# Partial chunks of keys filled up with zeros to 128 rows in two attentions' weighted sums of values

## The chip, the cores and the metric

The kernel runs on one core of a Trainium2 chip. The metric is the device time of one launch in microseconds (us); lower is better. The core's engines are called as in the profile: PE (TensorE) multiplies, and PEld is its loading of weights, which can overlap the multiplying; DVE (VectorE), ACT (ScalarE) and POOL (GpSimd) work on tiles; SP starts most of the transfers. Each engine takes its own instructions in order and waits for the others by semaphores.

## The reference, cut to what matters

A first layer (a gated delta rule with convolutions and an MLP) is followed by two layers of attention with squared-ReLU MLPs, over 528 tokens (16 meta tokens and 512 others). Only the two attentions are touched. The first is sparse: each query keeps its 256 best keys by an index (here as a bias of -1e30 on the others).

```
s = jnp.einsum('qgrd,qkgd->qgrk', q_blk, k_sel) * scale
s = jnp.where(valid[:, None, None, :], s, -jnp.inf)
p = jax.nn.softmax(s, axis=-1)
return jnp.einsum('qgrk,qkgd->qgrd', p, v_sel)      # the weighted sum of values
```

The second is the forgetting attention: 16 heads, all earlier keys, with a running sum of log decays in the logits, and again a softmax and a weighted sum of the values. Everything is float32, to float32 accuracy.

## The kernel before

Matmuls take float32r operands, each matrix split into a high and a low part (wh and wl of weights, xh and xl of inputs), or plain float32, where one product is two records in the trace. A matmul's shape in the trace begins with the active rows of the array and its columns: `64*128` has 64 rows, which is the number of keys over which it sums.

**Sparse attention** (`Dsa.attend`). An item is a block b of 32 tokens times 4 heads (128 queries on the partitions) and a group g of keys' heads; there are 17 blocks and 4 groups, so 68 items. `probs` makes logits on PE (L1315, L1316), adds bias and finds minima on DVE (L1318), and takes exponentials on ACT (L1323) into the tile `pr` [128 queries, keys], of which there are three buffers. `values`, two items later, transposes `pr` by chunks of 128 keys on PE (L1339), copies the transposes out of PSUM on ACT into `pT` (full chunks by L1342, a partial chunk by L1344), and sums weights times values over the chunks on PE (L1349). Block b sees 32 (b + 1) keys, so its last chunk has 32, 64, 96 or 128 rows in turn; the last block has 528 keys and a last chunk of 16. Blocks 0 to 3 have one chunk, 4 to 7 two, and so on. Meanwhile DVE still finds the best keys of the last rows (`index`, L1279 and L1280), PE does the output products of the first tokens (`out`, L99) from item 40 on, and at item 38 `finish` transposes factors (L182), copies them (L1060, ACT) and multiplies the residual by them in eight instructions on POOL (L1072).

**Forgetting attention** (`Fox.attend`). An item is a pair of heads j, a pair of query tiles u, a head of the pair `par` and a tile r of 128 queries. Keys are cut so that chunk 0 is the 16 meta tokens and the other four are 128 each. `values(j, u, par)` runs 8 x 2 x 2 = 32 times: it transposes weights of 256 queries (L1653, always 128 columns, of which chunk 0 uses 16), splits them into the tiles pTh and pTl (L106 on ACT, L107 on DVE), and multiplies both with the values `V` (L1664). `prepare` makes `V` of the next pair of heads, in two buffers. PE does products of the next pair of heads (L99) in between.

The order of each engine's instructions is set by a scheduler in the building of the program, from the order in the code, priorities and a model of times; it can change wherever an instruction is added.

Of the kernel before, what the change touches and what calls it, by code (L numbers as in the profile page):

```python
# [28 lines left out]
# chunks of tokens: the partitions of a column, where each starts and how many of its tokens count  # L29
# [4 lines left out]
# columns of the packed per-partition parameters  # L34
# [12 lines left out]
class K:  # L47
    """The kernel's context: engines, pools and the pieces that recur."""

    def __init__(self, tc):  # L50
        self.tc = tc
        self.nc = tc.nc
        self.whole = False  # whether a bank takes all the tokens where it can
        self.low = None  # the engine of the weights' lower parts

    def psum(self, **banks):
        """A pool of PSUM banks, so many a tag, for a phase."""
        self.banks = banks
        assert sum(banks.values()) <= 8
        return self.tc.tile_pool(name="pm", bufs=1, space=PSUM)  # L60
# [4 lines left out]
    # ---------------------------------------------------------------- dense  # L65
    def load(self, wdram, kt=8, m=128):
        """Loads a block of kt tiles of weights for m outputs."""
# [5 lines left out]
    def weights(self, wdram, kt=8):  # L73
        """A block of kt tiles of weights, split into two float32r parts that sum to it exactly."""
        return self.weight_parts(self.load(wdram, kt), kt)
# [10 lines left out]
    def dense(self, wdram, xh, xl, evac, kt=8, lo=0, n=T):  # L86
        """One block of 128 outputs for n tokens, a bank of them at a time: evac(products, tokens) takes them over."""
# [14 lines left out]
    def split(self, hi, lo, src, w=None):  # L102
        """hi + lo = src (times w, a value per partition)."""
# [8 lines left out]
    def operand(self):  # L112
        """Two float32r tiles for the parts of a layer's input; the last ones' readers are done."""
        return [self.big.tile([128, KT, T], F32R, name=n, tag=n) for n in ("bigh", "bigl")]

    def operand2(self):
        """Another such pair."""
# [6 lines left out]
    # ---------------------------------------------------------------- 1 / sqrt  # L124
    def rsqrt(self, pool, out, ms, scale, eps, shape, tag, bufs=2):
        """out = (ms * scale + eps) ** -0.5 by an integer first guess and three Newton steps."""
# [21 lines left out]
    def squares(self, tiles, pool=None, lo=0, eng=None):  # L148
        """Sums over the tiles of their squares from token lo on, [128, tokens] with zeros around."""
# [15 lines left out]
    def sumsq(self, acc, chunks):  # L165
        """The sums over the partitions too, as columns of PSUM (a column a chunk of tokens)."""
# [7 lines left out]
    def rows(self, cols, chunks, take, tags=("pa", "pa")):  # L174
        """The transposes of cols(chunk) [tokens, 128], to take(values, tokens)."""
# [26 lines left out]
def delta_constants(k, pool):  # L202
    nc = k.nc
    # tri[d][j, i] = 1 where token j counts in the running sum of token i
# [15 lines left out]
# -------------------------------------------------------------------- first layer  # L220
# blocks of w_in: a head's q, k, v, then z, sc_b, sc_c, sc_x, gate_a, gate_b
# [9 lines left out]
class Layer1:  # L231
# [13 lines left out]
    def normed(self, out, lo=0):  # L245
        """Takes over the products of the tokens from lo on with their norm."""
# [4 lines left out]
    def start(self):  # L251
        """The input times the norm's weights, the tokens' factors of the norm, which follow the products, and the first blocks."""
        k, nc, s, io, xh, xl = self.k, self.nc, self.s, self.io, self.xh, self.xl
        # where the recurrence's tiles will be
# [39 lines left out]
    def gates(self):  # L294
        """Log decays, their running sums by chunks and betas."""
# [7 lines left out]
        with tc.tile_pool(name="l1g", bufs=1) as pg:  # L303
            G = self.G  # rows 0..15 beta, 32..47 decay; no decay where there is no token
# [99 lines left out]
    # ---- towards the merge  # L404
    def load_u(self):
        """The convolved branch in two parts, where the recurrence's tiles were."""
# [16 lines left out]
    def sc_out(self, j):  # L423
        """2 sigmoid(gate_b) y_b for 128 features, in place of the gate."""
# [7 lines left out]
    # ---- independent of the recurrence  # L432
# [7 lines left out]
    def conv_branch(self, j):  # L440
        """sc_b * conv(sc_c * sc_x) for 128 features, in three steps."""
# [27 lines left out]
    # ---- gated delta rule  # L469
    def setup(self):  # L470
        k, nc, tc, p = self.k, self.nc, self.tc, self.p
        # masks of the blocks that the first level of the inverse adds, for Q = (W N)^T: block b of Q's columns keeps the
        # rows of the sibling of that block
# [15 lines left out]
        # tokens from NM - 4 on, and one of none  # L489
# [7 lines left out]
    def stage_a(self, h):  # L497
        """Projections, convolutions and silu of one head: 2 silu of k and q by chunks, and of v."""
# [3 lines left out]
        for kind in "kqv":  # L502
            x = self.xp[self.xi % 3]
            self.xi += 1
            # queries count from token NM on (and float32r takes an even number of tokens)
# [30 lines left out]
    def stage_b(self, h, st):  # L536
        """Token-major k and -v, decays, the triangular systems and the inverses of their diagonal blocks."""
# [64 lines left out]
    def levels(self, h, st):  # L602
        """The inverses, block by block, doubled up to the chunk's size."""
# [17 lines left out]
        # blocks of 16: W += W N W between siblings, by way of Q = (W N)^T with a mask  # L621
# [21 lines left out]
        def turn(d, rows, cols):  # L643
            """A block of V as the transpose of W's."""
# [5 lines left out]
        # larger ones start at partitions that a product can take by itself  # L650
        for lv in LEVELS[1:]:
# [3 lines left out]
            def products(d, out, rows, cols, lhs, rhs, eng, pairs=None):  # L655
                """out[rows, cols] = lhs^T rhs for the pairs of blocks."""
# [24 lines left out]
    def stage_c(self, h, st):  # L681
        """The recurrences over the chunks in both directions, the norm and the gate of the output."""
# [54 lines left out]
        # with o = sum / sqrt(128) rq:  o rsqrt(mean(o^2) + eps)  # L737
# [27 lines left out]
def softplus(k, pool, y, A, n):  # L765
    """max(y, 0) + log1p(exp(-|y|)), the log by the series of 2 atanh(e / (2 + e))."""
# [1004 lines left out]
def fcol(v):  # L1771
    """[n * 128] -> [128, n]"""
    return np.asarray(v, np.float32).reshape(-1, 128).T
# [81 lines left out]
```

## Time and profile before

| what | value |
|---|---|
| times of three runs | 2604.51, 2614.54, 2614.96 us (median 2614.54) |
| span of the profiled execution | 2607.7 us |
| busy share of the span | PE 97%, PEld 89%, DVE 59%, ACT 41%, POOL 17% |
| sparse attention, `attend` | about 1365 to 1493 us of the span |
| forgetting attention, `attend` | about 1994 to 2224 us |

The profiled execution is one of its own; its time beside the span is not among the three, and the median stands 6.8 us above that span. Times in the trace count from the start of the span. A matmul's end is modelled, so the step from one start to the next tells more than its length. A granted clock of 1.00 is 2.4 GHz, 0.50 is 1.2 GHz.

### The profile page before, as it was taken

The page shows a single profiled execution, that of the slowest core. Times are in us where ns is not written, and L with a number is a line of the kernel's source. Part 1 is how long each engine was busy: PE and PEld are TensorE (multiplying, and loading weights), DVE is VectorE, ACT ScalarE, POOL GpSimd, SP SyncE. Part 2 cuts the span into 40 slices and gives each one's busy share as a digit, 9 for nine tenths or more (in the row PEclk, how much of TensorE's full clock was granted, in tenths as well). Part 3 has the DMA queues.
Part 4 walks back from the last instruction along what each step waited for, and adds up shares of the span by engine and source line. Part 5 has one row for each costly group of instructions (what it writes and reads, how often), then busy time and mean ns, then how long its engine had stood idle before and what let it go on. Part 6 is the DMA issues. An engine that isn't in the chain of part 4 may idle for free.

```text
span 2607.7 us, 45619 instructions
## 1 busy us (share of the span) xinstructions
PE 2523.1 (97%) x18012; PEld 2315.5 (89%) x18012; DVE 1535.0 (59%) x3288; ACT 1072.2 (41%) x2191; POOL 438.4 (17%) x599
## 2 busy tenths in 40 slices
PE   8899999999999999999879999999999999999999
PEld 8889999999899888888868999999999988788887
DVE  7878788766554444335998454244555767642432
ACT  5434445353423322333546543133334766431331
POOL 2322212100002111013641010000112444100000
PEclk9999999999999999999978999999999989999999
DMA  4334333524552332333321232223333222232332
GB/s 152 94 95 121 84 96 90 118 89 133 169 204 89 97 97 92 96 90 109 87 71 39 62 114 90 90 89 95 119 95 97 83 72 65 90 95 91 97 105 81
DMA packets 139206, 257.20 MB, mean 99 GB/s; under 512 B 65536, under 2 KB 69664, under 8 KB 138992
## 3 DMA queue, kind: packets, MB, share of 16 engines
q1 hardware_dynamic: 82176, 236.46, 29.2%
q10 hardware_dynamic: 56816, 17.82, 3.5%
q8 instruction: 142, 2.33, 0.4%
q14 instruction: 72, 0.59, 0.1%
HBM read 223.39 MB, written 22.34 MB: 94 GB/s over the span
## 4 chain that ended last, share of the span: by engine, by line
PE 79%; DVE 11%; DMA 3%; ACT 2%; issue 1%; POOL 0%; ACTq 0%; SPq 0%; DVEq 0%; POOLq 0%
PE ps_pd L99 46%; PE ps_pd L948 19%; PE ps_pa L1349 2%; PE ps_po L1664 2%; PE ps_pb L662 1%; DVE prod L839 1%; DVE wl L83 1%; PE ps_pt L1653 1%; PE ps_pt L1339 1%; DVE sc L1280 1%; DVE sc L1268 1%; DMA Dn<-gsc 1%; DVE m L1279 1%; DVE t L1086 1%; DMA blk<-nd 1%
## 5 line engine op out<-in xcount | busy, mean ns | idle before, releaser
L82 ACT ACTIVATE wh<-wr 128x1024 fp32r<-128x1024 f32 (+2 forms) x367 | 379.4, 1034 | 966.7 <-PE ps_pd L99 470.1
L99 PE MATMUL ps_pd<-bigh,wh 128*128 128x256 f32 (+5 forms) x2256 | 695.5, 310 | 17.7 <-ACT bigh L109 6.5
L99 PE MATMUL ps_pd<-bigh,wl 128*128 128x256 f32 (+5 forms) x2256 | 692.5, 308 | 5.4 <-DVE wl L83 5.4
L99 PE MATMUL ps_pd<-bigl,wh 128*128 128x256 f32 (+5 forms) x2256 | 692.5, 308 | 1.2 <-DVE bigl L110 1.0
L83 DVE TENSOR_TENSOR wl<-wr,wh 128x1024 fp32r<-128x1024 f32 (+2 forms) x355 | 429.1, 1209 | 314.9 <-ACT wh L82 308.8
L99 PEld LDWEIGHTS ps_pd<-bigh,wh 128*128 128x128 f32 (+1 forms) x2256 | 430.8, 191 | 39.5 <-ACT bigh L109 6.7
L99 PEld LDWEIGHTS ps_pd<-bigh,wl 128*128 128x128 f32 (+1 forms) x2256 | 430.9, 191 | 24.0 <-DVE wl L83 6.8
L99 PEld LDWEIGHTS ps_pd<-bigl,wh 128*128 128x128 f32 (+1 forms) x2256 | 431.0, 191 | 20.4 <-DVE bigl L110 3.0
L99 PE MATMUL ps_pd<-xh,wh 128*128 128x264 f32 (+1 forms) x1040 | 327.4, 315 | 1.2 <-ACT t L1544 1.2
L99 PE MATMUL ps_pd<-xh,wl 128*128 128x264 f32 (+1 forms) x1040 | 326.4, 314 | 0.8 <-DVE wl L83 0.8
L99 PE MATMUL ps_pd<-xl,wh 128*128 128x264 f32 (+1 forms) x1040 | 325.8, 314 | 0.0
L948 PE MATMUL ps_pd<-fh,wh 128*128 128x264 f32 (+1 forms) x944 | 315.6, 334 | 0.0
L948 PE MATMUL ps_pd<-fh,wl 128*128 128x264 f32 (+1 forms) x944 | 315.6, 334 | 0.0
L948 PE MATMUL ps_pd<-fl,wh 128*128 128x264 f32 (+1 forms) x944 | 315.4, 334 | 0.0
L99 PEld LDWEIGHTS ps_pd<-xh,wh 128*128 128x128 f32 x1040 | 196.7, 189 | 13.8 <-ACT t L1544 2.1
L99 PEld LDWEIGHTS ps_pd<-xh,wl 128*128 128x128 f32 x1040 | 196.8, 189 | 12.7 <-DVE wl L83 1.3
L99 PEld LDWEIGHTS ps_pd<-xl,wh 128*128 128x128 f32 x1040 | 196.9, 189 | 11.7
L948 PEld LDWEIGHTS ps_pd<-fh,wl 128*128 128x128 f32 x944 | 177.2, 188 | 19.5
L948 PEld LDWEIGHTS ps_pd<-fh,wh 128*128 128x128 f32 x944 | 177.2, 188 | 19.5
L948 PEld LDWEIGHTS ps_pd<-fl,wh 128*128 128x128 f32 x944 | 177.3, 188 | 19.3
L163 POOL TENSOR_TENSOR acc<-acc,sq 128x512 f32<-128x512 f32 (+1 forms) x35 | 62.1, 1773 | 602.7 <-ACT sq L162 592.8
L857 DVE TENSOR_TENSOR h<-ps_pd,h 128x256 f32<-128x256 f32 (+3 forms) x112 | 56.2, 502 | 163.9 <-PE ps_pd L948 129.3
(448 smaller groups left out, 3944.2 us busy)
## 6 DMA issues: line engine op xcount, KB each, us to landing
wr<-wm SPq DMA_DIRECT2D x128, 512.0 KB
wr<-w SPq DMA_DIRECT2D x72, 512.0 KB
wr<-wgu SPq DMA_DIRECT2D x44, 512.0 KB
wr<-wa SPq DMA_DIRECT2D x17, 512.0 KB
wr<-wkv SPq DMA_DIRECT2D x17, 512.0 KB
wr<-wdn SPq DMA_DIRECT2D x16, 512.0 KB
wr<-wao SPq DMA_DIRECT2D x16, 512.0 KB
ck<-cd SPq DMA_DIRECT2D x16, 264.0 KB
```

The lines of the kernel that those rows point to most:

```text
L82: nc.scalar.activation(wh, wr, AF.Copy)
L83: (self.low or nc.vector).tensor_tensor(wl, wr, wh, ALU.subtract)
L99: nc.tensor.matmul(ps[:, :half], a[:, k], b[k][:, ts], start=(k == 0 and i == 0), stop=(k == kt - 1 and i == 2))
L163: (eng or nc.vector).tensor_tensor(acc, acc, sq, ALU.add)
L662: nc.tensor.matmul(pq[r, c, :w], lhs(pr)[:, c], rhs(pr)[:, c], start=True, stop=True)
L839: nc.vector.tensor_tensor(prod[:, :i, :i], X[:, :i, :i], bt[:, :i, i].rearrange("p (o j) -> p o j", o=1).broadcast_to([2 * H, i, i]), ALU.mult
L857: k.nc.vector.tensor_add(v, ps, v)
L948: nc.tensor.matmul(pss[h][:, :half], a[:, q], b[f0 + q][:, ts], start=(f0 + q == 0 and i == 0), stop=(f0 + q == nf - 1 and i == 2),)
L1086: nc.vector.tensor_tensor(t, t, sw, ALU.add)
L1268: nc.vector.scalar_tensor_tensor(acc[:n, c0:c1], rl[:n, : c1 - c0], wi[:n, i, hd : hd + 1], acc[:n, c0:c1], ALU.mult, ALU.add)
L1349: nc.tensor.matmul(O[b][:, g], pT[:m, c], self.V[:m, c, 64 * g : 64 * g + 64], start=(c == 0), stop=(c == nch - 1))
L1664: nc.tensor.matmul(po, V[: ns[c], c, par].rearrange("p a n -> p (a n)"), t[: ns[c], c - g], start=(c == 0 and t is hi), stop=(c == nch - 1 ...
```

## The change

In the sparse attention, where the last chunk of a block's keys is partial (not in the last block), `probs` sets the rest of the chunk in `pr` to zero on POOL, and `values` treats the chunk as full. A full last chunk needs no copy of its own, so L1342 takes all chunks of the item at once. In the forgetting attention, `prepare` sets all of chunk 0 of `V` to zero on POOL before the 16 rows of it are written, and the matmuls over chunk 0 take all 128 rows of `V` and of pTh and pTl. The last block of the sparse attention keeps its chunk of 16 rows.

```
             pr = s.tile([128, T], F32, name="pr", tag="t", bufs=3)
+            if N % 128 and N < 512:
+                nc.gpsimd.memset(pr[:, N : 128 * (N // 128 + 1)], 0.0)
             nc.scalar.activation(
...
         def values(b, g):
-            N = min(32 * (b + 1), T)
+            N = T if b == NBLK - 1 else 128 * (b // 4 + 1)
...
         V = s.tile([128, 5, 2, 2, 64], F32R, name="V", bufs=2)
+        nc.gpsimd.memset(V[:, 0].bitcast(F32), 0.0)
...
                         nc.tensor.matmul(
-                            po, V[: ns[c], c, par].rearrange("p a n -> p (a n)"), t[: ns[c], c - g],
+                            po, V[:, c, par].rearrange("p a n -> p (a n)"), t[:, c - g],
                             start=(c == 0 and t is hi), stop=(c == nch - 1 and t is lo),
                         )
```

Comments are blank lines in the changed file. Its lines from L1323 on stand two further, and from `prepare`'s memset on three, so that L1342 there is L1344.

The scheduler moves instructions. On ACT, at block 4 of the sparse attention (128 + 32 keys), there stood before:

```order
L1323 ACTIVATE pr,l<-lg,mn 128x160 x2
L1342 ACTIVATE pT<-ps_pt 128x128
L1344 ACTIVATE pT<-ps_pt 32x128
L1342 ACTIVATE pT<-ps_pt 128x128
L1344 ACTIVATE pT<-ps_pt 32x128
L1323 ACTIVATE pr,l<-lg,mn 128x160 x2
```

and there stands now, for the same two items, one copy each:

```order
L1325 ACTIVATE pr,l<-lg,mn 128x160 x2
L1344 ACTIVATE pT<-ps_pt 128x256 x2
L1325 ACTIVATE pr,l<-lg,mn 128x160 x2
L106 ACTIVATE bigh<-ps_pa 128x8x32
L1344 ACTIVATE pT<-ps_pt 128x256 x2
```

POOL had almost nothing in the sparse attention's items before (the selection of `sc` belongs to the index, the rows of `h` to `finish`):

```order
L1176 TENSOR_TENSOR S_12811<-t,S_12811 64x17x32
L1273 AFFINE_SELECT sc<-sc 112x112
L1072 TENSOR_TENSOR h<-h,bb 128x512 x8
L1293 MEMSET bb 128x528
L163 TENSOR_TENSOR acc<-acc,sq 128x528 x13
```

Now the memsets of `pr` stand among them, and those of block 10 (the first `128x32 x4` below the rows of `h`) come after seven of the eight multiplications:

```order
L1324 MEMSET pr 128x96 x4
L1324 MEMSET pr 128x64 x3
L1072 TENSOR_TENSOR h<-h,bb 128x512
L1324 MEMSET pr 128x64
L1072 TENSOR_TENSOR h<-h,bb 128x512 x7
L1324 MEMSET pr 128x32 x4
L1324 MEMSET pr 128x96 x4
L1324 MEMSET pr 128x64 x4
```

On PE the last chunks of block 10's first two items, which wait for those memsets, were transposed with the other chunks of their item before (`96x128`):

```order
L1349 MATMUL ps_pa<-V,pT 128x64 x3
L1339 MATMUL ps_pt<-idn,pr 128x128 x2
L1339 MATMUL ps_pt<-idn,pr 96x128
L1315 MATMUL ps_ps<-KH_12812,S_12808 128x384
L1316 MATMUL ps_ps<-KL_12816,S_12808 128x384
```

Now both stand together (`L1341 ... x2`), further on among the output products, 115 records of PE behind the second group of L182 that `finish` needs:

```order
L1315 MATMUL ps_ps<-KH_12813,S_12809 128x384
L1316 MATMUL ps_ps<-KL_12817,S_12809 128x384
L99 MATMUL ps_pd<-bigh,wl 128x256
L99 MATMUL ps_pd<-bigh,wh 128x256
L99 MATMUL ps_pd<-bigl,wh 128x256
L99 MATMUL ps_pd<-bigh,wl 128x256
L1341 MATMUL ps_pt<-idn,pr 128x128 x2
```

## Rows read from the trace of the kernel before

**Rows 1.** The page's chain that ended last, shares of the span by engine.
```profile
PE 79%; DVE 11%; DMA 3%; ACT 2%; issue 1%; POOL 0%; ACTq 0%; SPq 0%; DVEq 0%; POOLq 0%
```

**Rows 2.** Windows: length, busy us of PE, PEld, DVE, ACT, POOL, clock, DMA.
```profile
1366.00:1380.00 14.00, 13.98 (x53) 10.85 (x51) 7.24 (x32) 7.45 (x31) 0.28 (x1) 0.50 0.00 0
1395.00:1410.00 15.00, 14.82 (x117) 13.47 (x116) 14.37 (x54) 13.05 (x54) 0.00 (x0) 1.00 0.13 31
1410.00:1425.00 15.00, 15.00 (x116) 13.91 (x114) 13.50 (x36) 8.56 (x29) 10.09 (x8) 1.00 0.19 52
2020.00:2060.00 40.00, 40.00 (x315) 38.11 (x313) 28.90 (x89) 27.93 (x70) 18.25 (x38) 1.00 0.31 90
```

**Rows 3.** Timeline of PE, forgetting attention: start, length, engine, line, operation, rows*columns, shape.
```profile
2001.54 0.38 PE L1664 MATMUL ps_po<-pTh,V 16*128 16x256 f32 x1
...
2095.32 0.28 PE L99 MATMUL ps_pd<-xh,wl 128*128 128x264 f32 x1
2095.53 0.38 PE L1664 MATMUL ps_po<-pTh,V 16*128 16x256 f32 x1
2095.75 0.28 PE L1664 MATMUL ps_po<-pTl,V 16*128 16x256 f32 x1
2095.95 0.39 PE L1664 MATMUL ps_po<-pTh,V 128*128 128x256 f32 x1
2096.18 0.28 PE L1664 MATMUL ps_po<-pTl,V 128*128 128x256 f32 x1
2096.29 0.29 PE L1664 MATMUL ps_po<-pTh,V 128*128 128x256 f32 x1
...
2220.17 0.58 PE L1664 MATMUL ps_po<-pTh,V 16*128 16x256 f32 x1
```

**Rows 4.** Timeline of PE, sparse attention, full clock.
```profile
1398.38 0.28 PE L1316 MATMUL ps_ps<-KL,S 128*128 128x256 f32 x1
1398.58 0.43 PE L1349 MATMUL ps_pa<-V,pT 64*128 64x64 f32 x2
1398.95 0.39 PE L1315 MATMUL ps_ps<-KH,S 128*128 128x256 f32 x1
...
1402.95 0.33 PE L1349 MATMUL ps_pa<-V,pT 96*128 96x64 f32 x2
1403.10 0.38 PE L1315 MATMUL ps_ps<-KH,S 128*128 128x288 f32 x1
```

**Rows 5.** Timeline of PE, sparse attention, half clock.
```profile
1368.58 0.69 PE L1349 MATMUL ps_pa<-V,pT 32*128 32x64 f32 x2
1369.20 0.56 PE L1260 MATMUL ps_ps<-kih,qi 128*112 128x264 f32 x1
...
1383.70 0.53 PE L1349 MATMUL ps_pa<-V,pT 96*128 96x64 f32 x2
1383.98 0.56 PE L1315 MATMUL ps_ps<-KH,S 128*128 128x256 f32 x1
```

**Rows 6.** Windows of 3.4 us, columns as in rows 2.
```profile
1383.20:1386.60 3.40, 3.27 (x20) 2.82 (x20) 2.92 (x11) 2.46 (x12) 0.00 (x0) 0.82 0.00 0
...
2100.60:2104.00 3.40, 3.30 (x19) 2.83 (x18) 3.14 (x10) 2.55 (x5) 1.36 (x2) 0.59 0.42 117
2104.00:2107.40 3.40, 2.84 (x12) 2.55 (x13) 3.09 (x12) 2.11 (x5) 0.74 (x1) 0.50 0.63 143
2107.40:2110.80 3.40, 3.40 (x25) 3.13 (x24) 1.22 (x7) 1.03 (x5) 0.16 (x2) 0.90 0.00 0
```

**Rows 7.** Instructions by line: count, ns min/median/max, first and last start, forms.
```profile
L1344 ACT ACTIVATE pT<-ps_pt x52: 249/260/284, 1366.3 to 1491.5; 32x128 f32<-32x128 f32 x16, 64x128 f32<-64x128 f32 x16, 96x128 f32<-96x128 f32 x16, 16x128 f32<-16x128 f32 x4
L1659 POOL MEMSET pTl<- x32: 201/205/208, 1999.5 to 2221.8; 128x128 f32 x32
```

**Rows 8.** Timeline around `finish`, PE and POOL.
```profile
1414.02 0.48 PE L182 MATMUL ps_pt<-idn,rf 128*128 128x128 f32 x2
1414.91 10.99 POOL L1072 TENSOR_TENSOR h<-h,bb 128x512 f32<-128x512 f32 x8 [37.16 <-ACT bb L1060]
```

More of the change, by code (lines that the diff above doesn't have):

```diff
@@ L1322, in probs @@
             pr = s.tile([128, T], F32, name="pr", tag="t", bufs=3)
+            if N % 128 and N < 512:
+                nc.gpsimd.memset(pr[:, N : 128 * (N // 128 + 1)], 0.0)
             nc.scalar.activation(
@@ L1328, in values @@
         def values(b, g):
-            N = min(32 * (b + 1), T)
+            N = T if b == NBLK - 1 else 128 * (b // 4 + 1)
             pr = P.pop((b, g))
@@ L1559, in prepare @@
         V = s.tile([128, 5, 2, 2, 64], F32R, name="V", bufs=2)
+        nc.gpsimd.memset(V[:, 0].bitcast(F32), 0.0)
         for a, b in ((0, 1), (1, 5)):
@@ L1664, in values @@
                         nc.tensor.matmul(
-                            po, V[: ns[c], c, par].rearrange("p a n -> p (a n)"), t[: ns[c], c - g],
+                            po, V[:, c, par].rearrange("p a n -> p (a n)"), t[:, c - g],
                             start=(c == 0 and t is hi), stop=(c == nch - 1 and t is lo),
```

## The prediction

> **What bounds the kernel now.** I read the chain that ended last first: PE holds 79% of it, DVE 11% [rows 1]. So what PE spends or saves counts almost one for one, but the share is an average, and the change sits in two stages. I read windows of these next [rows 2]. In the forgetting attention PE is busy 40.00 of 40 us, with DVE at 28.90, ACT at 27.93 and POOL at 18.25: PE is the bound and nobody else is near. The sparse attention has three parts. At 1366 to 1380 us PE is busy 13.98 of 14 us, at a granted clock of 0.50, and DVE 7.24: PE bounds. At 1395 to 1410 DVE has 14.37 of 15 and PE 14.82: two engines share the end. From 1410 PE is full (15.00) again. The last reading is the timeline of PE around matmuls with few active rows, from one start to the next, since the ends are modelled.
>
> **What few rows cost.** In the forgetting attention a run of two 16-row matmuls takes .86 us from the start of the first (2095.32, the L99 before it included) to the start of the second 128-row one (2096.18): .21 + .22 + .20 + .23 over four steps. A step between 128-row matmuls is .11 to .12 (2096.18 to 2096.29) [rows 3]. So four steps without the change of rows would be .48, and the run costs .38 too much, at its entry and its exit. In the sparse attention at full clock, the 64-row group takes .20 to come in and .37 to be left (1398.38 to 1398.95 = .57). The 96-row group is left after .15 (1402.95 to 1403.10), and comes in with a step of .12 like any other; together .27 [rows 4]. So a group of 64 rows costs .30 and one of 96 costs nothing. At half clock the 32-row group is left after .62, where a 96-row one is left after .28 [rows 5]: at least .34, its entry not counted. My reading is that a weight load is hidden behind the matmul before it unless the two differ in the rows they use by more than a step from 128 to 96. What it is inside the array I can't tell; that the price goes with the change of rows is what the rows show.
>
> By the Trainium skill ("TensorE: Matmul & The Clock Gate", section "LDWEIGHTS (loading the stationary operand)") a weight load's time is set by its columns: "A 32×128 weight load takes the same time as a 128×128 weight load". By it filling up rows changes no time, and the sum would be 2614.5; the trace disagrees, with .57 against .27 us.
>
> **The change, part by part.**
>
> *Chunk 0 of the forgetting attention, 128 rows for 16.* There are 40 runs of 16-row matmuls, the first at 2001.54 and the last at 2220.17 [rows 3]: 32 calls, of which eight have the high and the low part apart. 40 x .38 = 15.2 us of PE. The matmul streams the same 256 columns either way. PE is full here, but when it needs 15 us less in 226, it waits oftener for ACT's and DVE's splits of the weights (28 and 29 of 40 busy). I take four fifths: 12.2 us. The bounds are 15.2 and a third of it, 5.1.
>
> *Partial chunks of the sparse attention.* L1344 copied 16 chunks of 32 rows, 16 of 64 and 16 of 96 [rows 7], so 32 groups change rows by enough to be paid for. Eight of them (blocks 0 and 1) lie at half clock: 8 x .34 = 2.7 us, where PE is full, all of it on the path. Twelve (blocks 4, 5, 8) lie where DVE's search is nearly full: 12 x .30 = 3.6, of which I take half, 1.8, with nothing and 3.6 as bounds. Twelve (blocks 9, 12, 13) lie after 1410, where PE is full: 3.6, all of it. The sum is 8.1 us. The transposes now produce 128 columns of zeros and weights instead of 32 to 96; the step of a 128-column transpose among its like is .11 to .12, as that of a 128-row matmul, so I count nothing, and 48 x .02 = 1 us as the upper bound.
>
> *One copy less on ACT.* In 36 items L1344 falls away beside L1342: 36 x .26 = 9.4 us less of ACT, less the longer copy. ACT is busy 7.45 of 14 and 8.56 of 15 us [rows 2], so it is no bound except at 1395 to 1410 (13.05 of 15). I count nothing; there it is one reason to take half and not less.
>
> *Memsets of `pr`.* The nearest row is the memset of 128x128 (L1659), .205 us [rows 7]. 48 memsets of at most 96 columns take at most 9.8 us of POOL, which is busy 0.28 of 14 there. The exponentials don't wait for them, only the transposes of the last chunk do, two items later. The cover is POOL's idleness, and it is missing in one place, at `finish`: the eight multiplications hold POOL for 10.99 us from 1414.91 [rows 8], and block 10's memsets are queued behind them. The transposes that wait for them stand 115 records of PE behind the L182 pair at 1414.02; at .12 a step PE gets there after 13.8 us, POOL is free after 1425.90 - 1414.02 = 11.9 us. The slack is 1.9 us, so I count nothing. If `finish` starts late, or PE passes those records faster, PE stands at the head of its queue with everything behind it: up to 3 us lost, and in the worst case, if the products are not ahead, the 11 us of POOL's run.
>
> *Memset of `V`.* Eight, 256 columns each, so twice L1659's at most: 8 x .41 = 3.3 us of POOL, with 18.25 of 40 busy. It is done a pair of heads ahead, in the other buffer. Nothing, 3.3 as the bound.
>
> *The clock.* The granted clock is 0.50 from before 1366 and rises within 1383.2 to 1386.6: with a mean of 0.82 it stood at half for .36 of the window, to about 1384.4 [rows 2, 6]. PE was busy all the while, but with steps that wait for weight loads; it rose after the first 96-row groups (1383.70 [rows 5]). In the forgetting attention it stands at half from about 2101.2 to 2108.1 (0.59, 0.50, 0.90 over three windows: 2.8 + 3.4 + .7 = 6.9 us [rows 6]), after PE had waited. Each us at half clock that becomes one at full saves .5. I expect that without the waits for loads it rises earlier in blocks 0 and 1: 6 us less at half, 3 us saved. The bounds are 0 and 10 (all the 18 us from 1366 on halved would be 9).
>
> **Sum:** 12.2 + 8.1 + 3 = 23.3 us off a profiled span of 2607.7, so a span near 2584. The median of the runs stands 6.8 above that span, and I take the same offset: 2614.5 - 23.3 = 2591. Its own range is 2579 (15.2 + 9.9 of PE and 10 of clock, 35 us) to 2600 (half of 15.2, the sparse 2.7 and 3.6 at blocks where PE is full, nothing from the clock: 13.9 us).
>
> **Rivals.**
>
> *A. The gain is absorbed.* PE's saving turns into waits for DVE and ACT: only the last twelve sparse groups' 3.6 and a third of 15.2 remain, 8.7 us: 2606. For it: DVE bounds 14.37 of 15 us at 1395, and a chain of splits with 70% busy can have latencies of its own. Against it: PE has no idle time at all in 2020 to 2060. Chance .15.
>
> *B. Rows don't matter.* The long steps belong to the change of kind (a float32 product of two records among float32r ones) or to the wait for the tile, and stay. Then it is 2614, give or take POOL's work. For it: 1398.38 to 1398.58 is .20 already, at the entry. Against it: the 96-row groups have the same change of kind and cost nothing. Chance .04. The rule of the Trainium skill cited above (same page and section) is this case too.
>
> *C. Slower: the clock falls oftener.* If a faster PE waits for splits once in each pair of heads as at 2104 (busy 2.84 of 3.40 [rows 6]), each fall costs 6.9 x .5 = 3.4 us. Seven more of them, one for each other pair of heads, cost 23.8; with rival A's 8.7 gained it is 2630. It ends on the slower side from three falls, which use up A's gain, and by a measurable amount from seven. For it: the clock did fall at such a place once. Against it: that place had a DMA share of .63, so PE had waited for transfers and not for splits. Chance .05.
>
> *D. More than forecast.* All of PE's 25.1 us count and the clock comes back by the first block: 2579. Chance .08.
>
> **How the numbers follow.** The forecast has .68, A .15, D .08, C .05, B .04. The range of 8 in 10 goes from 2578, just under D, to 2606, at A: it leaves out C, B and the half of A that lies above, .16. A measurement of this kernel tells about 0.5% (13 us) from no change, so faster means below 2601.5. The forecast lies there but for its tail (.68 less .03), D does, and a fifth of A: .76. B and the rest of A are within 0.5%: .19. C is slower: .05.
>
> **What the profile after would show.** If I am right, the step from a chunk-0 matmul (L1664, now L1667) to the next is .11 to .12 as between any others; a 64-row group's .57 becomes about .27; the copies of partial chunks are left only as 16x128; the sparse stage (1366 to 1493) is shorter by 8 to 11 us and the forgetting one (1994 to 2224) by some 12; the clock rises before 1384; no wait of PE on POOL of more than 2 us near `finish`. If A is right, PE shows idle time in 2020 to 2060 that ends on ACT or DVE. If C is right, there are more windows of that stage at 0.50. I am wrong if the steps stay long with 128 rows, if the reordering of PE puts an item's transposes ahead of its exponentials so that PE waits at places that were full, or if the stages after these two take back what these gain.

## The result and the profile after

The changed kernel takes 2585.06 us (median of four runs, 2583.22 to 2592.53); the kernel before took 2614.75 on the same occasion (2604.51 to 2618.51). The ratio is 0.9902, with a 95% interval of 0.9876 to 0.9927: about 26 us faster. (The two medians differ by 29.7 us, but the four runs of each spread over 9.3 and 14.0 us; the text goes by the ratio.) Timed once more on another occasion it was 0.9924 (0.9908 to 0.9939), about 20 us. The forecast was 2591, 23 us faster.

The head of the page after, and the chain that ended last by engine, which answers to [rows 1]:

```profile
span 2581.5 us, 45694 instructions
PE 2490.0 (96%) x18012; PEld 2295.8 (89%) x18012; DVE 1531.5 (59%) x3288; ACT 1068.4 (41%) x2155; POOL 447.6 (17%) x655
...
PE 78%; DVE 12%; DMA 5%; ACT 2%; issue 2%; POOL 1%; SPq 0%; ACTq 0%; DVEq 0%; POOLq 0%
```

The span fell by 26.2 us (2607.7 to 2581.5) with the same 18012 matmuls. To see where, I counted each stage from its first to its last matmul: the sparse attention from the first logits (L1315) to the last weighted sum (L1349, now L1351), the forgetting attention from the first transpose (L1653, now L1656) to the last weighted sum (L1664, now L1667). Windows with these ends, first of the kernel before, then of the changed one (length, then busy us of PE, PEld, DVE, ACT, POOL, clock, DMA):

```profile
1349.94:1492.93 142.99, 130.55 (x935) 118.72 (x933) 100.27 (x314) 86.75 (x282) 13.14 (x11) 0.89 0.19 55
1997.43:2222.63 225.20, 219.62 (x1589) 201.62 (x1587) 168.51 (x489) 153.58 (x379) 97.57 (x212) 0.95 0.27 76
```

```profile
1350.61:1483.71 133.10, 119.18 (x934) 112.80 (x933) 99.38 (x314) 85.19 (x246) 20.66 (x57) 0.92 0.20 59
1987.85:2197.86 210.01, 200.70 (x1588) 192.56 (x1587) 166.39 (x489) 152.49 (x379) 97.36 (x218) 0.98 0.30 82
```

The sparse stage lost 9.9 us and the forgetting stage 15.2, with the same number of matmuls in each but for a record: 25.1 of the 26.2 us lie there. In the forgetting stage PE's busy time fell by 18.9, so PE waits 3.7 us more than before (9.3 against 5.6). ACT made 36 instructions less in the sparse stage (282 to 246), POOL 46 more.

The steps themselves, on PE's timeline of the changed kernel: an item of block 5 in the sparse attention, whose second chunk had 64 rows before, and a matmul of L1667 in the forgetting attention among matmuls of other lines:

```profile
1390.91 0.38 PE L1341 MATMUL ps_pt<-idn,pr 128*128 128x128 f32 x2
1391.12 0.64 PE L1351 MATMUL ps_pa<-V,pT 128*128 128x64 f32 x4
1391.60 0.40 PE L1341 MATMUL ps_pt<-idn,pr 128*128 128x128 f32 x2
...
2030.11 0.28 PE L99 MATMUL ps_pd<-xh,wh 128*128 128x264 f32 x1
2030.23 0.28 PE L1667 MATMUL ps_po<-pTh,V 128*128 128x256 f32 x1
2030.35 0.38 PE L182 MATMUL ps_pa<-idn,re 128*128 128x128 f32 x2
```

The four records of block 5's two chunks take .48 us in all, .12 each, where the 64-row group alone took .57 from its entry to its exit [rows 4]. The steps into and out of L1667 are .12 us, where the run of 16 rows had four of .20 to .23 [rows 3]. None of the 40 runs of 16 rows is left.

The windows that answer to [rows 2], and two around the clock's rise, which answer to [rows 6]:

```profile
1366.00:1380.00 14.00, 13.75 (x78) 12.53 (x79) 10.62 (x50) 10.15 (x48) 1.56 (x10) 0.70 0.00 0
1395.00:1410.00 15.00, 14.52 (x121) 13.55 (x120) 14.52 (x47) 10.75 (x35) 1.16 (x7) 1.00 0.09 21
1410.00:1425.00 15.00, 15.00 (x130) 15.00 (x129) 13.03 (x29) 9.14 (x21) 12.36 (x13) 1.00 0.31 95
2020.00:2060.00 40.00, 39.55 (x322) 38.32 (x321) 31.73 (x86) 30.76 (x73) 19.99 (x43) 1.00 0.33 93
1371.00:1374.40 3.40, 3.40 (x18) 3.22 (x18) 1.97 (x8) 2.25 (x12) 0.28 (x2) 0.50 0.00 0
1374.40:1378.00 3.60, 3.58 (x27) 3.22 (x26) 3.24 (x16) 2.90 (x14) 0.65 (x4) 0.99 0.00 0
```

In the first 14 us PE now gets through 78 matmuls instead of 53. The clock rises at 1374.4, where it rose at 1384.4; the first weighted sum began at nearly the same time (1367.64 before, 1368.35 now).

### The profile page after: what moved, and what is told of

Read it like the earlier page. It is cut to its first block, busy times and chain, and to the rows that moved or that the text cites. A ratio compares the mean times of both kernels' runs of the same rounds, so it can differ in the third digit from the quotient of the medians.

```text
span 2581.5 us, 45694 instructions
## 1 busy us (share of the span) xinstructions
PE 2490.0 (96%) x18012; PEld 2295.8 (89%) x18012; DVE 1531.5 (59%) x3288; ACT 1068.4 (41%) x2155; POOL 447.6 (17%) x655
## 3 DMA queue, kind: packets, MB, share of 16 engines
q1 hardware_dynamic: 82176, 236.46, 29.7%
## 4 chain that ended last, share of the span: by engine, by line
PE 78%; DVE 12%; DMA 5%; ACT 2%; issue 2%; POOL 1%; SPq 0%; ACTq 0%; DVEq 0%; POOLq 0%
PE ps_pd L99 46%; PE ps_pd L948 19%; DVE wl L83 1%; PE ps_pa L1351 1%; PE ps_po L1667 1%; PE ps_pb L662 1%; DMA wd<-Xt 1%; DVE prod L839 1%; PE ps_pt L1656 1%; DVE sc L1280 1%; DVE t L1086 1%; PE ps_pt L1341 1%; DVE sc L1268 1%; DVE m L1279 1%; DMA Dn<-gsc 1%
## 5 line engine op out<-in xcount | busy, mean ns | idle before, releaser
L99 PE MATMUL ps_pd<-bigh,wh 128*128 128x256 f32 (+5 forms) x2256 | 693.3, 309 | 17.4 <-ACT bigh L109 6.5
L99 PE MATMUL ps_pd<-bigh,wl 128*128 128x256 f32 (+5 forms) x2256 | 690.9, 307 | 5.2 <-DVE wl L83 5.2
L99 PE MATMUL ps_pd<-bigl,wh 128*128 128x256 f32 (+5 forms) x2256 | 690.1, 307 | 0.9 <-DVE bigl L110 0.8
L99 PEld LDWEIGHTS ps_pd<-bigh,wh 128*128 128x128 f32 (+1 forms) x2256 | 428.8, 190 | 38.9 <-ACT bigh L109 6.5
L99 PEld LDWEIGHTS ps_pd<-bigh,wl 128*128 128x128 f32 (+1 forms) x2256 | 428.6, 190 | 23.4 <-DVE wl L83 6.5
L99 PEld LDWEIGHTS ps_pd<-bigl,wh 128*128 128x128 f32 (+1 forms) x2256 | 428.6, 190 | 20.0 <-DVE bigl L110 2.6
L99 PE MATMUL ps_pd<-xh,wh 128*128 128x264 f32 (+1 forms) x1040 | 326.4, 314 | 0.5 <-ACT t L1546 0.3
L99 PE MATMUL ps_pd<-xh,wl 128*128 128x264 f32 (+1 forms) x1040 | 325.6, 313 | 0.5 <-DVE wl L83 0.5
L99 PE MATMUL ps_pd<-xl,wh 128*128 128x264 f32 (+1 forms) x1040 | 325.0, 313 | 0.0
L99 PEld LDWEIGHTS ps_pd<-xh,wh 128*128 128x128 f32 x1040 | 196.1, 189 | 12.9 <-ACT wh L82 0.6
L99 PEld LDWEIGHTS ps_pd<-xh,wl 128*128 128x128 f32 x1040 | 196.2, 189 | 12.1 <-DVE wl L83 1.0
L99 PEld LDWEIGHTS ps_pd<-xl,wh 128*128 128x128 f32 x1040 | 196.2, 189 | 11.5
```

The costliest lines, as they stand in the source:

```text
L99: nc.tensor.matmul(ps[:, :half], a[:, k], b[k][:, ts], start=(k == 0 and i == 0), stop=(k == kt - 1 and i == 2))
```

## The experiments

The table has all runs. "Half" is the time in the stage at a granted clock of 0.50, by the trace's record of the clock. Stage times are us, from one profiled execution each; the ratio is that to the kernel before, timed beside it, with its 95% interval.

| kernel | ratio (interval) | sparse stage, half | forgetting stage, half |
|---|---|---|---|
| before | 1 | 143.0, 30.7 | 225.2, 23.9 |
| changed | 0.9902 (0.9876 to 0.9927) | 133.1, 20.5 | 210.0, 6.8 |
| changed, again | 0.9924 (0.9908 to 0.9939) | 133.1, 20.5 | 211.5, 10.2 |
| fox_only | 0.9939 (0.9924 to 0.9954) | 143.6, 34.1 | 209.9, 0.0 |
| dsa_only | 0.9963 (0.9948 to 0.9977) | 132.3, 17.1 | 228.3, 20.5 |
| copy_only | 1.0020 (1.0009 to 1.0031) | 150.5, 47.8 | 225.1, 20.5 |
| apart | 1.0043 (1.0026 to 1.0059) | 143.6, 34.1 | 235.5, 23.9 |
| rows96 | 0.9888 (0.9861 to 0.9916) | 132.3, 20.5 | 212.9, 13.7 |
| rows96, again | 0.9904 (0.9889 to 0.9920) | 131.5, 20.5 | 208.5, 0.0 |
| rows64 | 1.0012 (1.0000 to 1.0025) | 142.3, 30.7 | 226.3, 17.1 |
| dve_fill | 0.9914 (0.9891 to 0.9938) | 132.6, 17.1 | 212.1, 17.1 |
| stack | 0.9922 (0.9900 to 0.9944) | 133.0, 20.5 | 213.5, 17.1 |
| fill_last | 0.9905 (0.9891 to 0.9920) | 131.8, 20.5 | 210.6, 10.2 |
| no_lo | 0.9918 (0.9902 to 0.9935) | 133.1, 20.5 | 211.1, 17.1 |

How far a stage's length varies by itself, kernels tell whose engines have the same order of instructions in it: the forgetting stage took 225.2 and 228.3 us (before and dsa_only), 208.5 and 212.9 (rows96 twice), 210.0, 211.5 and 210.6 (changed twice, fill_last). So a difference of 4 us between single profiles of that stage says little. The sparse stage agrees with itself within 1.3 us. There the five profiles of kernels that keep few rows stood at half clock for 30.7 to 47.8 us and the nine with filled rows for 17.1 to 20.5: the earlier rise of the clock goes with the filled rows.

My theory: a change of the rows in use between two matmuls, from 128 to 64 or fewer or back, exposes the weight load, and the change takes these away. Rivals: the 36 copies saved on ACT or the new order of the instructions made the gain; the clock made it; few rows as such are slow.

**fox_only** is the kernel before with the forgetting attention's edits alone:

```
+        nc.gpsimd.memset(V[:, 0].bitcast(F32), 0.0)
...
-                            po, V[: ns[c], c, par].rearrange("p a n -> p (a n)"), t[: ns[c], c - g],
+                            po, V[:, c, par].rearrange("p a n -> p (a n)"), t[:, c - g],
```

> Only the forgetting attention's part of the change (the memset of V and chunk 0 with 128 rows). Stage lengths are counted from the first to the last matmul of a stage: before 143.0 us in the sparse attention (first L1315 to last L1349) and 225.2 in the forgetting one (first L1653 to last L1664); changed kernel 133.1 and 210.0. If the price is that of rows: the forgetting stage 208 to 213 us, no step between chunk 0 and its neighbours above 0.13 us at full clock, the sparse stage as before (141 to 145, 64-row groups still left after 0.57), and about 0.6 of the gain, 14 to 18 us. If the gain was made by the clock alone (it fell less often in the changed kernel by chance of its schedule), the stage stays above 218 while the granted clock is at half as often as before.

Its stage's window:

```profile
1999.73:2209.63 209.90, 198.77 (x1588) 189.97 (x1587) 166.58 (x489) 153.19 (x379) 99.98 (x218) 1.00 0.29 82
```

209.9 us, and the sparse stage as before (143.6): the part's whole gain, 0.61% of the time. But the clock was at full speed in all of that stage, so this kernel alone doesn't part rows from clock. Its comparison with rows64, below, is the closest.

**dsa_only** is the other half: the memset of `pr` and the full chunks (`N = T if b == NBLK - 1 else 128 * (b // 4 + 1)` in `values`).

> Only the sparse attention's part (memsets of pr, full chunks, one copy). If the price is that of rows: sparse stage 131 to 135 us, the forgetting stage 223 to 227 with runs of 16 rows that cost 0.38 as before, and 9 to 11 us less than before in all. If the two parts only help each other through the order, neither alone gives its share.

132.3 us in the sparse stage and 228.3 in the forgetting one, a little above what was expected. The two ratios less one add up to 0.98%, and the whole change gave 0.98% and 0.76%: within the intervals the parts add up.

**copy_only** has dsa_only's memsets, transposes and merged copies, but the matmuls keep their few rows:

```
             for c in range(nch):
-                m = min(128, N - 128 * c)
+                m = min(128, min(32 * (b + 1), T) - 128 * c)
                 nc.tensor.matmul(O[b][:, g], pT[:m, c], self.V[:m, c, 64 * g : 64 * g + 64], start=(c == 0), stop=(c == nch - 1))
```

> The sparse attention with memsets, full transposes and one copy for all chunks, as in the change, but its matmuls still take only the 32, 64 or 96 rows that hold weights; the forgetting attention as before. If the price is that of rows, the sparse stage stays near 143 us (140 to 145) and the 32- and 64-row groups still cost about 0.57 in and out. If what helped was the 36 copies that ACT no longer makes, or the new order of the instructions, the stage falls to 131 to 135 us as in the change.

No gain from the copies or the order, and more than that: the stage is 7.5 us longer than before. Its window as a whole, and around a place where the clock, having risen, fell again:

```profile
1349.47:1499.94 150.47, 137.79 (x934) 126.16 (x933) 102.08 (x314) 86.03 (x246) 20.67 (x57) 0.84 0.17 52
...
1386.70:1390.10 3.40, 3.38 (x24) 2.64 (x23) 3.25 (x15) 2.71 (x12) 0.69 (x4) 1.00 0.02 5
1390.10:1393.60 3.50, 3.25 (x21) 2.67 (x21) 2.79 (x10) 2.49 (x12) 0.30 (x2) 0.99 0.15 35
1393.60:1407.20 13.60, 13.60 (x58) 12.43 (x58) 7.68 (x27) 5.80 (x23) 0.65 (x5) 0.50 0.07 15
```

The 17.1 us more at half clock (47.8 against 30.7) go with the 7.5 us, but the order of the instructions differs from that of the kernel before as well, so the 7.5 us need not be the clock's alone. While the clock was down PE was busy without a gap by the profile (13.60 of 13.60); before the fall it had waited .25 us of 3.5. Why the clock stayed down longer and fell once more is not settled: the kernel before has the same groups of few rows in its blocks 4 and 5, and its clock stood at full speed there. So this kernel shows that the copies and the order don't make the gain; what the copies are worth by themselves rows96, below, tells better.

The closest comparison is with the changed kernel itself. In this stage copy_only has its order of instructions on PE, DVE and POOL, and on ACT but for one copy; only the rows in the weighted sums differ. With few rows the stage takes 150.5 us, with filled ones 133.1 (dsa_only, again in the same order: 132.3). So at one order the rows are worth 17 to 18 us here, the earlier rise of the clock included (47.8 against 20.5 and 17.1 us at half), and with few rows the new order, with its memsets and merged copies, was the slower one.

**apart** doubles the suspected cost in the kernel before, with the same matmuls:

```
+                order = [(c, t) for c in cs for t in (hi, lo)]
+                if g == 0:
+                    order = [order[0], order[2], order[1], order[3]]
-                for c in cs:
-                    for t in (hi, lo):
+                for c, t in order:
```

> The kernel before, but in each call of the forgetting attention's values the second matmul of chunk 0 stands behind the first of chunk 1, so that rows go 16, 128, 16, 128 where they went 16, 16, 128, 128: the number of 16-row runs rises from 40 to about 64 with the same work. If each change of rows is paid for: 24 x 0.38 = 9 us longer there, 231 to 237 us where there were 225. If few rows as such are slow, or the kind of matmul is, nothing changes: 223 to 227.

The trace counts 64 runs of 16 rows, as meant. The stage's window, and one call on PE's timeline (each `x2` of L1667 is a 16-row and a 128-row matmul):

```profile
1997.48:2232.94 235.46, 229.18 (x1589) 204.95 (x1587) 169.93 (x489) 154.63 (x379) 96.95 (x212) 0.95 0.26 73
...
2027.69 0.28 PE L99 MATMUL ps_pd<-xh,wh 128*128 128x264 f32 x1
2027.91 0.70 PE L1667 MATMUL ps_po<-pTh,V 16*128 16x256 f32 x2
2028.53 0.69 PE L1667 MATMUL ps_po<-pTl,V 16*128 16x256 f32 x2
2029.07 0.28 PE L1667 MATMUL ps_po<-pTh,V 128*128 128x256 f32 x1
```

Five steps take 1.38 us (2027.69 to 2029.07), where five of .12 are .60: .78 too much, two runs at .39. The stage is 10.3 us longer at the same time at half clock; 24 x .38 = 9.1 were expected. It is the change of rows that is paid for, and PE bounded that stage in the kernel before: all of a cost added there arrived in the time.

**rows96 and rows64** fill up to 96 and to 64 rows only; chunk 0 takes as many. Of the first:

```
             N = min(32 * (b + 1), T)
+            if 0 < N % 128 < 96 and N < 512:
+                N = 128 * (N // 128) + 96
...
-                            po, V[: ns[c], c, par].rearrange("p a n -> p (a n)"), t[: ns[c], c - g],
+                            po, V[: max(ns[c], 96), c, par].rearrange("p a n -> p (a n)"), t[: max(ns[c], 96), c - g],
```

> Partial chunks of 32 and 64 rows in the sparse attention are filled to 96 rows, not 128, so they keep a copy of their own on ACT and no copies are saved; chunk 0 of the forgetting attention takes 96 rows. If a weight load is hidden again as soon as no more than 32 rows are missing: 131 to 136 us in the sparse stage (before 143.0, changed kernel 133.1), 208 to 213 in the forgetting stage (before 225.2, changed kernel 210.0). If full chunks were needed for the gain: 143 and 225.

> The same with 64 rows: chunks of 32 become 64, chunks of 64 and 96 stay, and chunk 0 of the forgetting attention takes 64 rows for 16. If the price is one for any change to 64 rows or fewer, as the 32- and 64-row groups of the kernel before say: no gain, 141 to 146 and 223 to 228 us. If the price goes by the rows that are missing (112 missing at 16, 64 at 64 rows), the forgetting stage falls to about 217 to 220.

One call of `values` in the kernel with 96 rows (from the second profile of it), and then one in that with 64:

```profile
2024.98 0.29 PE L99 MATMUL ps_pd<-xh,wh 128*128 128x264 f32 x1
2025.10 0.28 PE L1669 MATMUL ps_po<-pTh,V 96*128 96x256 f32 x1
2025.22 0.28 PE L1669 MATMUL ps_po<-pTl,V 96*128 96x256 f32 x1
2025.34 0.28 PE L1669 MATMUL ps_po<-pTh,V 128*128 128x256 f32 x1
```

```profile
2028.22 0.28 PE L99 MATMUL ps_pd<-xh,wh 128*128 128x264 f32 x1
2028.43 0.38 PE L1669 MATMUL ps_po<-pTh,V 64*128 64x256 f32 x1
2028.65 0.28 PE L1669 MATMUL ps_po<-pTl,V 64*128 64x256 f32 x1
2028.86 0.38 PE L1669 MATMUL ps_po<-pTh,V 128*128 128x256 f32 x1
2029.08 0.28 PE L1669 MATMUL ps_po<-pTl,V 128*128 128x256 f32 x1
```

From L99's start to the second chunk's first matmul it is .36 us over three steps at 96 rows and .64 at 64; to the fourth, .86 at 64 rows, exactly the .86 of [rows 3] at 16. So there is a step somewhere above 64 and up to 96 rows, and no slope: 64 rows cost as much as 16. The times follow: with 96 rows the whole gain (131.5 and 132.3; 208.5 and 212.9), with 64 rows none. rows64 and fox_only have the same order in the forgetting stage, on ACT, DVE and POOL throughout and on PE but for one record, and differ there in chunk 0's 64 or 128 rows alone: 226.3 us (17.1 at half) against 209.9 (none at half). The clock does not make that difference: with the same 17.1 us at half dve_fill, stack and no_lo took 211.1 to 213.5. In rows96 ACT makes all its 282 instructions in the sparse stage, so the saved copies are worth nothing that can be seen.

> The kernel with 96 rows once more, in more rounds. If 96 rows hide a weight load as well as 128 and the copies that the change saves on ACT are worth nothing: the same time as the changed kernel within 0.3%. If the saved copies are worth something after all: slower than the changed kernel by over 0.3%.

The medians of that occasion were 2582.88 (96 rows) and 2589.17 (128 rows), with overlapping intervals. The profiled spans were 2582.5 and 2591.7. The trace of the latter began the sparse stage at 1360.20 us and that of the former at 1352.67, with the same work before it, so 7.5 of these 9.2 us came from ahead of the change. I call the two the same.

> The changed kernel once more, beside the next three on the same chip: sparse stage 132 to 134 us, forgetting stage 209 to 213 (other kernels with the same two stages had 209.9 to 212.9), and 0.988 to 0.993 of the time before.

133.1 and 211.5 us, and 0.9924: all as expected.

The records of the weight loads (PEld) show whether it is the load that is exposed. Around the run of [rows 3] in the kernel before, and then in the kernel with 96 rows:

```profile
2095.20 0.19 PEld L99 LDWEIGHTS ps_pd<-xh,wl 128*128 128x128 f32 x1
2095.52 0.18 PEld L1664 LDWEIGHTS ps_po<-pTh,V 16*128 16x128 f32 x1
2095.63 0.18 PEld L1664 LDWEIGHTS ps_po<-pTl,V 16*128 16x128 f32 x1
2095.95 0.19 PEld L1664 LDWEIGHTS ps_po<-pTh,V 128*128 128x128 f32 x1
2096.06 0.19 PEld L1664 LDWEIGHTS ps_po<-pTl,V 128*128 128x128 f32 x1
```

```profile
2024.98 0.19 PEld L1669 LDWEIGHTS ps_po<-pTh,V 96*128 96x128 f32 x1
2025.10 0.19 PEld L1669 LDWEIGHTS ps_po<-pTl,V 96*128 96x128 f32 x1
2025.22 0.19 PEld L1669 LDWEIGHTS ps_po<-pTh,V 128*128 128x128 f32 x1
```

A load takes .18 us with 16 rows and .19 with 128, so it is its start that moves. Among equal rows a load starts .11 to .12 us after the one before it, and as much ahead of its own matmul. At a change between 128 and 16 rows it starts .32 us after the one before it, at the start of its own matmul (2095.52 and 2095.53, 2095.95 and 2095.95): it is no longer hidden behind the matmul before. At full clock all 72 changes between 16 and 128 rows at L1664 took .307 us or more from load to load; of the 80 between 96 and 128 rows in the second profile of rows96, 72 took .135 or less. In the sparse attention of the kernel before the same step was .25 to .26 us at most changes to and from 32 and 64 rows.

**dve_fill** writes the zeros of `pr` on DVE (`nc.vector.memset` for `nc.gpsimd.memset`).

> The changed kernel with the memsets of pr on DVE in place of POOL. If POOL's idle time was a cover that mattered: the 48 memsets lengthen DVE's queue where DVE bounds, 1 to 4 us of the sparse stage's gain is lost (134 to 137 us). If the memsets are too short to matter anywhere, 132 to 134. The forgetting stage stays at 209 to 211.

132.6 and 212.1 us: no loss. DVE's busy time in the stage rose from 99.4 to 101.1 us, so 46 of the fills cost it 1.7 us in all. POOL's idle time is no cover that is needed; the work is too small to matter.

**stack** uses the free rows. In the changed kernel it puts the lower part of chunk 0's weights into rows 32 to 47 of `pTh`, and one matmul takes both:

```
+                nc.scalar.activation(V[32:48, 0], V[:16, 0], AF.Copy)
...
+                    nc.scalar.activation(hi, pt, AF.Copy)
+                    nc.vector.tensor_tensor(lo[:, 1], pt[:, 1], hi[:, 1], ALU.subtract)
+                    nc.vector.tensor_tensor(hi[32:48, 0], pt[:16, 0], hi[:16, 0], ALU.subtract)
...
-                    for t in (hi, lo):
+                    for t in (hi, lo) if c else (hi,):
```

> The changed kernel, with the free rows of chunk 0 in the forgetting attention used: the lower parts of its 16 weights go to rows 32 to 47 of the tile with the upper ones, V has the same 16 rows there once more, and one matmul takes both where there were two. PE has 32 matmuls of 0.12 us less, 3.8 us; DVE gets one more small instruction in each of 32 calls, ACT one in each pair of heads. If PE still bounds that stage: 206 to 208 us there (changed kernel 210.0). If the splits on ACT and DVE have taken over, 209 to 213.

**no_lo** only leaves those 32 matmuls out, and adds nothing anywhere.

> The changed kernel, with the 32 matmuls of the lower part of chunk 0's weights left out of the forgetting attention (a term of the sum is missing then, about one part in thousands of chunk 0's share). PE has 3.8 us less to do there and no other engine has more. If PE still bounds the stage: 206 to 207.5 us, and the stacked kernel lost its gain to the instruction that it adds on DVE. If the splits of the weights on ACT and DVE now bound: 209 to 213, as stacked.

Their windows of the forgetting stage, stack first:

```profile
1988.28:2201.73 213.45, 200.46 (x1557) 192.42 (x1555) 171.58 (x521) 156.36 (x386) 98.99 (x218) 0.96 0.30 81
```

```profile
1989.28:2200.34 211.06, 201.95 (x1557) 193.18 (x1555) 167.42 (x489) 153.60 (x379) 100.28 (x218) 0.96 0.30 82
```

213.5 and 211.1 us, with 32 matmuls less and no gain to be seen: DVE's 5.2 us more in stack are not the only reason. Taking PE work away did not shorten the stage, while adding some to the kernel before lengthened it in full. That is less than a proof that the 3.8 us are worth nothing: both profiles had 17.1 us at half clock, at which dve_fill took 212.1, and the ratios of no_lo and of the changed kernel on that occasion, 0.9918 and 0.9924, can't tell 3.8 us (0.15%). The changed kernel's PE waits about 9.3 us there (210.01 less 200.70), by the view of waits mostly in short ones for the weights' splits (`pTl`, `pTh`), for `lr` and for `o`, and no_lo's clock was at half for 17.1 us. Which of the two, the waits or the clock, holds the stage at 210, these runs don't part.

**fill_last** adds to the changed kernel the last block's 16-row chunk:

```
+            if rem:
+                nc.gpsimd.memset(pT[:, nf], 0.0)
...
-                nc.tensor.matmul(O[b][:, g], pT[:m, c], self.V[:m, c, 64 * g : 64 * g + 64], start=(c == 0), stop=(c == nch - 1))
+                nc.tensor.matmul(O[b][:, g], pT[:, c], self.V[:, c, 64 * g : 64 * g + 64], start=(c == 0), stop=(c == nch - 1))
```

> The changed kernel, with the last block's chunk of 16 keys filled up too (the rest of that chunk of pT and of V set to zero on POOL, 128 rows in its four matmuls). Entry and exit of a 16-row group cost 0.25 + 0.25 us there where 0.11 + 0.11 is usual, so 4 x 0.28 = 1.1 us less if each is paid: 131 to 132.5 us in the sparse stage; too little for the ratio to tell from the changed kernel. A wait for the memset would show as idle time of PE behind POOL in the last items.

```profile
1355.70:1487.53 131.83, 118.15 (x934) 112.46 (x933) 99.14 (x314) 85.11 (x246) 21.52 (x61) 0.92 0.21 59
```

1.3 us less in the stage (131.8 against 133.1), PE's busy time 1.0 us less: as forecast, but dsa_only, without this edit, already took 132.3, so only .5 us lie outside the stage's own variation. Of the .25 to .26 us steps at 16 rows its trace has none. In the total it is not to be told from the changed kernel.

## Why the prediction was right

**What few rows cost** held in every number: .38 a run (.39 in apart), nothing at 96 rows, the full price at 64 and fewer. Rival B is out: a step of the weight loads is .12 or .32 us by the rows of the neighbour, with the same kind of matmul. The Trainium skill says ("TensorE: Matmul & The Clock Gate", section "LDWEIGHTS (loading the stationary operand)") that a load's time doesn't depend on its rows. The trace agrees as to the load itself, .18 us at 16 rows and .19 at 128; the forecast of no gain that the prediction drew from it fails, since that rule is about the load's length and not about its start.

**Chunk 0.** Forecast 12.2 us, all for the rows; the stage lost 15.2. At the same 17.1 us at half clock, 64 rows took 226.3 and dve_fill's 128 rows 212.1: 14.2 us for the rows. But the order differs between these two, and the stage varies by 3 to 4 us in one order, so the 15.2 of the whole count and the four fifths that I took are not told apart. The clock came down from 23.9 to 6.8 us at half. The prediction counted no gain from it here, and of the three stretches at half in the kernel before (from 2101.2, 2132.0 and 2210.5) it read the first alone. It was worth little: among the kernels whose rows are filled and that do the same work, the stage took 208.5 and 209.9 at none, 210.0 at 6.8, 210.6 and 211.5 at 10.2, 212.9 at 13.7 and 212.1 at 17.1. That is about .2 us for each us at half, not the .5 of the prediction, though the orders differ here too; that a slower PE only shortened its waits for others is my guess and not shown. Rival A, the absorbing by other engines, did not decide the forecast. Whether it is there at all stays open: PE waited 3.7 us more, but dsa_only, which has the order of the kernel before in this stage, waited 9.1 us as well; and a further 3.8 us of PE showed no gain.

**Partial chunks.** 8.1 us for the rows and 3 for the clock, 11.1 in all, were forecast; the stage lost 9.9. The starts of the first weighted sums of blocks show where: from block 0 to block 4 the kernel before took 21.44 us (1367.64 to 1389.08) and the changed one 16.30 (1368.35 to 1384.65), 5.1 less, against 2.7 for the eight groups and the clock's share. From block 4 to block 9 (1419.45 and 1413.55) it gained 1.5 us, against 1.8 for the twelve groups beside DVE's search; from there to the end 3.3, against 3.6. The clock's time at half fell by 10.2 us, not 6. What a us at half is worth in this stage, kernels of the same order show: 143.6 us at 34.1 (fox_only, apart) against 143.0 and 142.3 at 30.7 (before, rows64), and 133.0 to 133.1 at 20.5 (changed twice, stack, no_lo) against 132.3 at 17.1 (dsa_only), which is .2 to .4 us each and not .5. For 10.2 us it makes 2 to 4 us, and 2.7 for the rows would leave 2.4 to it; so the forecast fits, but in blocks 0 to 3 the two shares are not parted.

**The sum** came nearer than its parts: 3.0 us too little in the forgetting stage and 1.2 too much in the sparse one. That they partly cancel is luck.

**One copy less, memsets.** Counted at nothing, and copy_only, rows96 and dve_fill show nothing. My bounds for POOL were too high: these are the fills by size and line (count, busy us, mean ns), of `pr` and of `V`:

```profile
L1324 POOL MEMSET pr<- 128x96 f32 x16 | 2.8, 177 | 41.3 <-PE ps_pt L1341 39.9 <-DVE KL L1216 0.7 <-DVE S L1176 0.7
...
L1562 POOL MEMSET V<- 128x256 f32 x8 | 2.5, 314 | 0.0
L1324 POOL MEMSET pr<- 128x64 f32 x16 | 2.4, 151 | 21.3 <-PE ps_pt L1341 21.0 <-ACT pT L1344 0.2
L1324 POOL MEMSET pr<- 128x32 f32 x16 | 1.9, 125 | 14.5 <-PE ps_pt L1341 13.6 <-ACT pT L1344 0.9
```

That is 9.6 us in all, where the bounds were 9.8 + 3.3. At `finish` the slack was thinner than I said. On POOL and PE:

```profile
1410.09 1.29 POOL L1072 TENSOR_TENSOR h<-h,bb 128x512 f32<-128x512 f32 x1 [4.05 <-ACT bb L1060]
1411.32 0.15 POOL L1324 MEMSET pr<- 128x64 f32 x1
1411.42 10.72 POOL L1072 TENSOR_TENSOR h<-h,bb 128x512 f32<-128x512 f32 x7
1422.08 0.24 POOL L1324 MEMSET pr<- 128x32 f32 x3
...
1423.11 0.38 PE L1341 MATMUL ps_pt<-idn,pr 128*128 128x128 f32 x2
```

The first three of block 10's four fills ended at 1422.32, and the transposes that needed the first two came at 1423.11: .8 us of slack where 1.9 were worked out. PE was not kept waiting.

**Rival C** had no place: in the forgetting stage the clock fell twice, for 3.4 us each, where it had fallen three times. The offset between the profiled span and the median of the runs moved from 6.8 us to 3.6. Of either only some 1.7 us are steady (2583.22 for the execution with the span of 2581.5, and much the same in the other runs); the rest is scatter of the runs, so that the 6.8 in the forecast did no harm was luck. The total is 20 to 26 us by the two occasions, the forecast 23.3.

## What to carry to other kernels

On PE's timeline look at the steps where the number of active rows changes, not at the matmuls' lengths: here a change between 128 rows and 64 or fewer cost about .15 to .2 us at entry and again at exit, and 96 rows cost nothing. Then look at the weight loads: a load that starts with its own matmul, and not ahead of it, is exposed. Where such matmuls stand between full ones on a PE that is full, fill the operands up with zeros (to 96 rows is enough), or put the short ones side by side so that the change is paid once. Once PE has been relieved, take the next reading anew: a further 3.8 us of PE work showed no gain. To tell what an edit is worth, compare kernels in which the scheduler left the same order.

## What the runs showed that I had not expected

There is no slope between 16 and 64 rows: a run took .86 us at either. A load of 16 rows takes as long as one of 128, but starts .2 us later. The memsets, full transposes and merged copies, with few rows kept in the matmuls, made the sparse stage 7.5 us slower, with another order and 17.1 us more at half clock, though PE had the same number of matmuls. A us at half clock cost .2 to .4 us there, not .5. And the time from the start to the sparse attention, with the same work in all kernels, ranged from 1346.62 to 1360.20 us between profiles: the stages' own lengths (143.0 to 143.6, and 132.3 to 133.1 in the five profiles of kernels with the change's own sparse attention) tell these changes apart far better than the whole time.
